# First token block by features: W_in rows and modulation columns in feature order, six GLU chunks side by side

## The chip, the cores and the metric

The kernel runs on one core of one Trainium2 chip. The metric is the device time of one execution in microseconds (us). The engines are TensorE (PE, matrix products; PEld are its weight loads), VectorE (DVE), ScalarE (ACT), GpSimd (POOL) and SyncE (SP, which issues most transfers). Each engine works through its own list of instructions in order.

## The reference

One decoder layer over 4096 tokens of 1024 features in float32 (`x` is 1 x 4096 x 1024, `c` a vector of 1024):

```python
mod = silu(c) @ w_ada + b_ada                       # 3 x 1024
shift, scale, gate = split(mod, 3)
h = layer_norm(x) * (1 + scale) + shift
u_a, z_a, glu_b, z_b = split(h @ w_in + b_in)       # 512, 512, 1024, 512 columns
pooled = causal_multiscale_pool(u_a)                # windows 2, 4, 8, 16, less the token itself
y_a = (group_linear(pooled, w_pool) + b_pool) * ls_pool * silu(z_a)
v = glu_b[..., :512] * sigmoid(glu_b[..., 512:])
v = causal_depthwise_conv31(v, w_dw) + b_dw
v = silu(layer_norm(v) * ln_conv_g + ln_conv_b)
y_b = (v @ w_pw + b_pw) * silu(z_b)
y = concat(y_a, y_b) @ w_out + b_out
out = layer_norm(alpha * x + gate * y) * ln_post_g + ln_post_b     # alpha = 2 ** 0.25
```

## The kernel before

**Tiles.** The tokens are cut into 8 blocks of 512 ("token blocks", 0 to 7; `sb` in the code). Features are cut into 8 pieces of 128 (`k`), and W_in's 2560 columns into 20 chunks of 128 (`n0`): 0 to 3 are u_a, 4 to 7 z_a, 8 to 11 and 12 to 15 the two halves of the GLU, 16 to 19 z_b. To keep float32 accuracy each operand of a product is split into a high and a low part (`split`: ACT rounds to the high part, another engine subtracts), and `mm3` makes three matmuls of 128 x 128 by 128 x 512 for each feature piece (high by high, high by low, low by high).

**Phase 1.** It loads `c`, the vectors and the columns of `w_ada`, makes shift and scale (`mod_block`: 8 `macc` instructions of DVE and a few tiny matmuls for each 256 features), turns token block 0 on PE (`make_xT`), and then makes, for each token block, four GLU pairs (chunks 8+m and 12+m, m = 0 to 3) and the chunks 16 and 17 of z_b. The weights come as column chunks (`win_chunk`: 512 KB, runs of 512 bytes); for ten of them POOL makes the low part, where the later ones have DVE do it. The modulated and split x of each block goes to DRAM (`xD`), v to `vD`. `row_stats`, `norm_T` and `mod_xT` make the x of the next token block, while PE works on the current one.

**Phase 2.** For each token block xD is loaded again (POOL's queue), and PE makes `p2z` and `p2u` for four groups and `p2b` for the chunks 18 and 19. DVE makes the pooled means (`us`, `pp`) of each group from u.

**The convolution.** It runs on DVE beside phases 1 and 2. `conv(m, s0, n, ...)` handles 128 channels of n token blocks from s0, with 31 taps folded into about 46 instructions on even and odd tokens: into `cx` (even taps) and `ca` (the result). The blocks are (0,1), (1,2), (3,2), (5,1), called block 0, 1, 3 and 5 here; token blocks 6 and 7 follow as "late units" (`la`, `lx`, `lv`) in phases 2 and 3. After the four channel groups of a block, `conv_ln` makes its LayerNorm: transposes on PE into PSUM (`cl`), statistics on ACT and DVE, a power on POOL (`ccs`), a transpose of the statistics (`ccp`), a round trip through DRAM (`cD`, read back as `cbc`), two DVE passes over `ca`, stores to `tD`. It is called after the first channel group of the next block, at high priority.

**Phase 3.** For each token block `prep` loads the normalized convolution result, applies SiLU and splits it (`vp`), and splits y_a (`ya`); `pw_stage` makes the pointwise product (`pw`) and y_b; `out_tile` makes the output product (`po`, W_out times the gate in `wor`, `wo`), the last LayerNorm and the stores.

**What sets the order.** The tiles come from pools of buffers by tag; the buffers of a tag are handed out in the order of the program text, and a tile waits until its buffer's last user is done. The tags that matter here:

- "ca", 6 buffers: `ca`, `cx`, `lx`, `vp` (and `w_ada` at the start)
- "s2b", 2 PSUM banks (`s2_bank`): `cl`, `ccp`, and in the text of before also the GLU pair m = 2 of token block 0 and `fold_u`
- "acc", 4 PSUM banks (`acc_bank`): the other products; "tpb", 2 banks: transposes and `pw`
- "wraw", 2 buffers: weights before they are split

Among the instructions whose buffers allow it, a scheduler that simulates a timeline when the program is built sets one fixed order for each engine, so work that stands late in the text (convolution, late units, phase 3) is threaded between the work of the phases.

Of the kernel before, what the change touches and what calls it, by code (L numbers as in the profile page):

```python
# [39 lines left out]
def tile_layer(ctx, tc, x, x_t, w_in_t, c, w_ada, b_ada, w_in, b_in, w_pool, b_pool, ls_pool, w_dw, b_dw,  # L40
# [75 lines left out]
    nc.vector.tensor_copy(cols, vps[:, :NV])

    wrows = s2.tile([P, P], F32, tag="cto", bufs=2, name="wrows", padded_shape=[P, T])
    nc.scalar.dma_start(wrows[: CW * MC, :], w_dw.rearrange("j o (m p) -> (j o m) p", p=P))
    wps = tp_bank("wps")  # L120
    transpose(wps[:, : CW * MC], wrows[: CW * MC, :])
# [21 lines left out]
    def wada_block(b):  # L143
        tiles = []
        for q in range(4):
            if b == 0:
                wt = wp.tile([P, 2, 2, 2 * P], F32, tag=("whi", "wlo")[q % 2], bufs=10, name=f"wa{b}_{q}")
            elif b == 1:
                wt = xp.tile([P, 2, 2, 2 * P], F32, tag="x2", bufs=12, name=f"wa{b}_{q}")
            else:  # L150
# [7 lines left out]
            tiles.append(wt)
        return tiles

    def mod_block(b, wts):
        acc = s2.tile([P, 2, 2 * P], F32, tag="bc", bufs=2, name=f"macc_{b}", padded_shape=[P, 2, DH])
        last = None
        for kt in range(KT):
            src = wts[kt // 2][:, kt % 2]
            if kt == 0:
                nc.vector.tensor_scalar(acc, src, sc[:, 0:1], None, op0=ALU.mult)
            else:
                last = nc.vector.scalar_tensor_tensor(acc, src, sc[:, kt : kt + 1], acc,
                                                      op0=ALU.mult, op1=ALU.add)  # L170
        ps = tp_bank(f"mod{b}")
        for i in range(2):
            for j in range(2):
                nc.tensor.matmul(ps[:, 2 * i + j : 2 * i + j + 1], acc[:, 1 - i, j * P : (j + 1) * P],
                                 ones[:, 0:1], start=True, stop=True)
# [4 lines left out]
        nc.vector.tensor_scalar(shn[:, k0 : k0 + 2], shc[:, k0 : k0 + 2], -1.0, None, op0=ALU.mult)  # L180
        return last

    def split(hi, lo, src, eng=nc.vector):
        nc.scalar.copy(hi, src)
        eng.tensor_tensor(lo, src, hi.bitcast(F32), op=ALU.subtract)
# [554 lines left out]
```

## Time and profile before

| | |
|---|---|
| runs | 1399.49, 1400.14, 1400.76 us; median 1400.14 |
| the profiled execution | its span is 1404.7 us, from the first to the last instruction; no other time of it is given; 4.6 us above the median |
| PE busy | 1357.8 us (97%) |
| DVE busy | 1193.9 us (85%) |
| ACT, POOL busy | 431.7 us (31%), 167.2 us (12%) |
| DMA | 243.82 MB, mean 174 GB/s |
| mean clock granted to PE | 0.991 |
| phase 1, 2, 3 on PE | first p2z at 501.26 us, first pw at 955.37 us |

Busy time is the sum of the durations of an engine's instructions; overlapping neighbours make a sum a little larger than the time they took. A row of a timeline gives the start, the duration, the engine, the line of the program, the operation, out<-in, and in brackets the idle time before it and what ended that. The lines (L333 and so on) are lines of the kernel whose profile is shown.

### The profile page before, as it was taken

The numbers are of one execution on the slowest core, as the hardware profiler recorded it, in microseconds if no ns is written. First come the engines' busy times: TensorE is split into PE (matmuls) and PEld (weight loads), VectorE is DVE, ScalarE is ACT, GpSimd is POOL, SyncE is SP. The second block draws the span as 40 slices with busy tenths as digits, with TensorE's granted clock in tenths as the row PEclk, the third lists the DMA queues.
The fourth block names the chain that finished last, engine by engine and source line by source line (L and its number), as shares of the span: only waits on it lengthen the run. The fifth ranks groups of instructions, "written<-read, shape, count | busy, mean of one in ns | idle before, by whom it ended". The sixth has DMA issues, their size and how long they took to land.

```text
span 1404.7 us, 17113 instructions
## 1 busy us (share of the span) xinstructions
PE 1357.8 (97%) x6044; PEld 1118.6 (80%) x6044; DVE 1193.9 (85%) x2318; ACT 431.7 (31%) x764; POOL 167.2 (12%) x203
## 2 busy tenths in 40 slices
PE   3989999999999999999999999989999999999997
PEld 2878888888788888888888888778888888888886
DVE  7669999983479999899898699979897899998654
ACT  3535335344531322311114111434134131322310
POOL 4310000000100011110011110410111101001111
PEclk9999999999999999999999999989999999999999
DMA  9778776567474563361440741455444443433511
GB/s 313 235 279 312 257 276 241 173 255 242 162 253 151 174 210 124 111 202 42 161 166 31 239 136 61 136 183 173 161 173 138 155 158 122 157 128 122 191 62 75
DMA packets 119496, 243.82 MB, mean 174 GB/s; under 512 B 15026, under 2 KB 52722, under 8 KB 119410
## 3 DMA queue, kind: packets, MB, share of 16 engines
q1 hardware_dynamic: 109952, 209.07, 43.4%
q0 software_dynamic: 9216, 33.56, 7.2%
q8 instruction: 47, 0.77, 0.2%
q14 instruction: 39, 0.32, 0.1%
q10 hardware_dynamic: 242, 0.10, 0.0%
HBM read 156.65 MB, written 86.04 MB: 173 GB/s over the span
## 4 chain that ended last, share of the span: by engine, by line
PE 87%; DVE 4%; DMA 4%; ACT 2%; POOL 1%; issue 1%; SPq 1%; DVEq 0%; ACTq 0%
PE po L647 25%; PE p L335 6%; PE p L334 6%; PE p L333 6%; PE p2u L333 4%; PE p2u L334 4%; PE p2u L335 4%; PE p2z L333 4%; PE p2z L335 4%; PE p2z L334 4%; PE pw L623 2%; PE pw L625 2%; PE pw L624 2%; PE p2b L333 2%; PE p2b L335 2%; PE p2b L334 2%
## 5 line engine op out<-in xcount | busy, mean ns | idle before, releaser
L510 DVE SCALAR_TENSOR_TENSOR cx<-cv,wdw,cx 128x513 f32<-128x513 f32 (+1 forms) x240 | 144.6, 611 | 0.7
L510 DVE SCALAR_TENSOR_TENSOR ca<-cx,wsum,ca 128x256 f32<-128x256 f32 (+1 forms) x240 | 143.1, 608 | 0.1
L510 DVE SCALAR_TENSOR_TENSOR ca<-cv,wdw,ca 128x256 f32<-128x256 f32 (+1 forms) x224 | 133.5, 608 | 0.0
L676 POOL TENSOR_TENSOR ors<-ove,mhalf 128x1 f32<-128x1 f32 x32 | 46.3, 1447 | 409.3 <-DVE ove L672 400.9
L326 POOL DMA_DIRECT2D x2r<-xD x64 | 34.5, 540 | 402.7 <-PE p2b L335 276.4
L670 ACT ACTIVATE ojk<-r,osm 128x1024 bf16<-128x1024 f32 x31 | 35.6, 1149 | 148.3 <-DVE osm L667 148.3
L665 DVE SCALAR_TENSOR_TENSOR r<-po,r 128x512 f32<-128x512 f32 x62 | 40.8, 685 | 23.3 <-PE po L647 23.3
L510 DVE SCALAR_TENSOR_TENSOR lx<-lv,wdw,lx 128x257 f32<-128x257 f32 x120 | 57.2, 477 | 0.0
L510 DVE SCALAR_TENSOR_TENSOR la<-lx,wsum,la 128x256 f32<-128x256 f32 x120 | 57.0, 475 | 0.0
L451 ACT ACTIVATE sz<-p2z,cols 128x512 f32<-128x512 f32 x32 | 22.0, 687 | 108.0 <-PE p2z L335 108.0
L263 POOL TENSOR_TENSOR xcs<-smx,mhalf 128x1 f32<-128x1 f32 x28 | 19.2, 688 | 290.7 <-DVE smx L262 263.9
L297 ACT ACTIVATE x<-xk,shc 128x512 fp32r<-128x512 f32 x56 | 38.5, 721 | 47.5 <-DVE xk L288 46.1
L510 DVE SCALAR_TENSOR_TENSOR la<-lv,wdw,la 128x256 f32<-128x256 f32 x112 | 52.9, 475 | 0.0
L286 DVE TENSOR_TENSOR xk<-xk,xbc 128x1024 f32<-128x1024 f32 x28 | 34.0, 1220 | 16.7 <-DMA xk<-in_x_t_dram 16.5
L263 POOL TENSOR_TENSOR ccs<-smc,mhalf 128x1 f32<-128x1 f32 x32 | 37.2, 1169 | 91.9 <-DVE smc L262 91.2
L298 DVE SCALAR_TENSOR_TENSOR x<-xk,shc,x 128x512 fp32r<-128x512 f32 x56 | 40.4, 744 | 8.1 <-ACT x L297 8.1
L458 ACT ACTIVATE u<-p2u,bu 128x512 f32<-128x512 f32 x32 | 22.0, 689 | 75.6 <-PE p2u L335 75.6
L679 DVE SCALAR_TENSOR_TENSOR r<-r,ors,b_bc 128x1024 f32<-128x1024 f32 (+1 forms) x33 | 41.0, 1246 | 3.2 <-POOL ors L676 3.1
L647 PE MATMUL po<-wo0h,ya 128*128 128x512 f32 x128 | 41.2, 392 | 0.0
L647 PE MATMUL po<-wo1h,ya 128*128 128x512 f32 x128 | 41.1, 390 | 0.0
L259 ACT ACTIVATE x<-x 128x1024 f32<-128x1024 f32 x28 | 29.6, 1059 | 35.7 <-DMA x<-in_x_dram 35.2
L639 DVE SCALAR_TENSOR_TENSOR r<-r,gbo 128x1024 f32<-128x1024 f32 x32 | 38.9, 1217 | 1.8 <-DMA r<-in_x_dram 1.8
(356 smaller groups left out, 4137.8 us busy)
## 6 DMA issues: line engine op xcount, KB each, us to landing
x2r<-xD POOLq DMA_DIRECT2D x64, 512.0 KB, 7.8
xD<-x SPq DMA_DIRECT2D x56, 512.0 KB, 6.9
x<-in_x_dram SPq DMA_DIRECT2D x32, 512.0 KB, 7.9
r<-in_x_dram SPq DMA_DIRECT2D x32, 512.0 KB, 4.4
out_dram<-r SPq DMA_DIRECT2D x31, 512.0 KB, 2.6
xk<-in_x_t_dram SPq DMA_DIRECT2D x28, 512.0 KB, 6.5
wa<-in_w_ada_dram SPq DMA_DIRECT2D x32, 256.0 KB, 4.8
wr<-in_w_in_dram SPq DMA_DIRECT2D x16, 512.0 KB, 6.5
```

Of the source, the lines that this page charges most:

```text
L263: nc.gpsimd.tensor_tensor(rstd, sm[:, 2:3], mhalf[:, 0:1], op=ALU.pow)
L297: nc.scalar.activation(h2[:, 0, :], z, AF.Identity, bias=shc[:, k : k + 1])
L298: nc.vector.scalar_tensor_tensor(h2[:, 1, :], z, shc[:, k : k + 1], h2[:, 0, :].bitcast(F32), op0=ALU.add, op1=ALU.subtract)
L333: nc.tensor.matmul(ps, wh, X[0], start=first, stop=False)
L334: nc.tensor.matmul(ps, wh, X[1], start=False, stop=False)
L335: nc.tensor.matmul(ps, wl, X[0], start=False, stop=last)
L510: nc.vector.scalar_tensor_tensor(dst, src, wt, dst, op0=ALU.mult, op1=ALU.add)
L639: xg = nc.vector.scalar_tensor_tensor(r, r, ALPHA, gbo, op0=ALU.mult, op1=ALU.add)
L647: mm = nc.tensor.matmul(po[h], lhs, Wo[k][wi][:, h * 512 : (h + 1) * 512], start=(k == 0 and wi == 0 and lhs is yh), stop=last)
L665: nc.vector.scalar_tensor_tensor(r[:, sl], po[h], 1.0, r[:, sl], op0=ALU.mult, op1=ALU.add, accum_out=sm[:, h : h + 1])
L676: nc.gpsimd.tensor_tensor(rs, ve, mhalf[:, 0:1], op=ALU.pow)
L679: nc.vector.scalar_tensor_tensor(r[:, sl], r[:, sl], rs, b_bc[:, sl], op0=ALU.mult, op1=ALU.add)
```

## The change

1. At first only `b_ada` and `b_in` are loaded (2 transfers on ACT's queue). The other vectors, `w_dw` and the correction constants come after token block 0's products (`late_vectors`, on SP's queue).
2. The shift and scale columns of `w_ada` come in five blocks of 1, 1, 2, 2 and 2 feature pieces in place of four blocks of 2, into other buffers.
3. The GLU weights come as 8 rows of 128 features by 1024 columns (`load_row`, runs of 4 KB) in place of 8 column chunks, and are split row by row, in two pieces of 768 and 256 columns. The chunks of z_b that phase 1 needs come as two tiles (`Wz`).
4. All these low parts are made on DVE.
5. Token block 0: for each feature piece, six GLU chunks (8, 12, 9, 13, 10, 14) take their three products one after the other, in four banks of "acc" and two of "s2b". The pair m = 3 and z_b follow.
6. Token block 7, the last of phase 1: z_b first, then the pair m = 0, then the pairs 1, 2 and 3 side by side, the pair m = 2 in the two banks of "s2b".
7. The buffers of the gate and of `gbo` hold W_in rows first.

```diff
-    for nm, src, n in (("b_ada", b_ada, 24), ("b_in", b_in, 20), ("b_pool", b_pool, 4),
-                       ...
-        nc.scalar.dma_start(vrows[r0 : r0 + n, :], view)
+    load_cols((("b_ada", b_ada, 24), ("b_in", b_in, 20)), nc.scalar.dma_start, "a")
...
-    def split(hi, lo, src, eng=nc.vector):
+    def split(hi, lo, src):
         nc.scalar.copy(hi, src)
-        eng.tensor_tensor(lo, src, hi.bitcast(F32), op=ALU.subtract)
+        nc.vector.tensor_tensor(lo, src, hi.bitcast(F32), op=ALU.subtract)
...
-    def load_pair(m):
-        W[8 + m] = win_chunk(8 + m, nc.gpsimd)
-        W[12 + m] = win_chunk(12 + m, nc.gpsimd)
-
-    wad = [wada_block(0)]
-    load_pair(0)
+    def load_row(k):
+        home = k % 4
+        rows[k] = (wraw(f"wr{k}") if home < 2 else
+                   cst.tile([P, D], F32, tag=("gate", "gbo")[home - 2], name=f"wr{k}"))
+        nc.sync.dma_start(rows[k], w_in[k * P : (k + 1) * P, 8 * P : 16 * P])
+
+    mods = ((0, 1), (1, 1), (2, 2), (4, 2), (6, 2))
+    wad = []
+    for b, (k0, nk) in enumerate(mods):
+        wad.append(wada_tiles(b, k0, nk))
+        for k in range(k0, k0 + nk):
+            load_row(k)
...
     xT = []
-    for b in range(4):
-        if b < 3:
-            wad.append(wada_block(b + 1))
-            load_pair(1 + b)
-        last = mod_block(b, wad[b])
-        xT += make_xT(0, xt_next, range(2 * b, 2 * b + 2))
+    first = (8, 12, 9, 13, 10, 14)
+    pss0 = [acc_bank(f"p1_0_{n0}") for n0 in first[:4]] + [s2_bank(f"p1_0_{n0}") for n0 in first[4:]]
+    starts = {k0: b for b, (k0, nk) in enumerate(mods)}
+    mod_block(0, *mods[0], wad[0])
+    pb = turn_x(xt_next, 0)
+    for k in range(KT):
+        xT.append(mod_turned(pb, k))
+        split_cols(k, 0, 3)
+        split_cols(k, 3, 4)
+        if k + 1 < KT:
+            if k + 1 in starts:
+                b = starts[k + 1]
+                last = mod_block(b, *mods[b], wad[b])
+            pb = turn_x(xt_next, k + 1)
+        for n0, ps in zip(first, pss0):
+            mm3(ps, W[n0][k], xT[k], k == 0, k == KT - 1)
+    late_vectors()
...
     for sb in range(NSB):
...
-        for m in range(MC):
-            pa, pg = inproj(xT, (W[8 + m], W[12 + m]), f"p1_{sb}_{m}",
-                            s2_bank if sb == 0 and m == 2 else acc_bank)
...
+        if sb + 1 == NSB:
+            z_half(sb, xT)
+            glus(sb, (0,), xT, (acc_bank,) * 2)
+            glus(sb, (1, 2, 3), xT, (acc_bank,) * 2 + (s2_bank,) * 2 + (acc_bank,) * 2)
+            break
+        if sb == 0:
+            for m in range(3):
+                glu(0, m, pss0[2 * m], pss0[2 * m + 1])
+        for m in range(3 if sb == 0 else 0, MC):
+            glus(sb, (m,), xT, (acc_bank,) * 2)
```

The change also moves instructions that no line of the diff names. The rows below are the fixed order of one engine: line, operation, out<-in, size. A number behind a name's parts is a buffer number (`cl0_2_6720` is the transpose tile 2 of convolution block 0's LayerNorm; `p1_5_3_1` is token block 5, m = 3, second of the pair; `p1_7_15` in the changed kernel is token block 7, chunk 15; `ca5_3` is block 5, channel group 3; `us7_3_0` is token block 7, group 3).

PE, LayerNorm of convolution block 0. Before, rows 1452 to 1458 of PE, in token block 5's GLU of phase 1 (its first transposes are rows 479 and 480):

```order
L334 MATMUL p1_5_3_1_2831<-x2_5_6_2607,w15h_553 128x512
L77 MATMUL cl0_2_6720<-ident_75,ca0_0_6412 128x128
L77 MATMUL cl0_2_6720<-ident_75,ca0_1_6469 128x128
L77 MATMUL cl0_2_6720<-ident_75,ca0_2_6526 128x128
L77 MATMUL cl0_2_6720<-ident_75,ca0_3_6583 128x128
L77 MATMUL cl0_3_6731<-ident_75,ca0_0_6412 128x128
L77 MATMUL cl0_3_6731<-ident_75,ca0_1_6469 128x128
```

After, rows 1982 to 1984, the end of phase 1 and the start of phase 2, followed shortly by the transposes (rows 1998 to 2003):

```order
L337 MATMUL p2z_0_0_3743<-x2r_0_5_3737,w4h_3669 128x512
L338 MATMUL p2z_0_0_3743<-x2r_0_5_3737,w4h_3669 128x512
L73 MATMUL cl0_0_6731<-ident_75,ca0_0_6445 128x128
L73 MATMUL cl0_0_6731<-ident_75,ca0_1_6502 128x128
L73 MATMUL cl0_0_6731<-ident_75,ca0_2_6559 128x128
L73 MATMUL cl0_0_6731<-ident_75,ca0_3_6616 128x128
```

The last GLU product of phase 1 (`p1_7_15`) is row 1982 and the first `p2z` row 1983, so the transposes of block 0 moved from phase 1 into phase 2.

DVE, the convolution in phase 1. After, rows 507 to 513: the last tap of `cx1_1` is row 509, and the next instruction of a convolution is row 627, behind block 0's LayerNorm (rows 616 to 625):

```order
L576 SCALAR_TENSOR_TENSOR cx1_1_6798<-cv1_1_6796,wdw_99,cx1_1_6798 128x513
L268 TENSOR_SCALAR smx23_2307<-smx23_2307 128x1
L576 SCALAR_TENSOR_TENSOR cx1_1_6798<-cv1_1_6796,wdw_99,cx1_1_6798 128x513 x9
L445 SCALAR_TENSOR_TENSOR v4_1_2437<-p1_4_9_2385,cols_92,sg4_1_2435 128x512
L292 TENSOR_TENSOR xk5_0_2320<-xk5_0_2320,xbc5_2318 128x1024
L294 SCALAR_TENSOR_TENSOR xk5_0_2320<-xk5_0_2320,s1_281,xbc5_2318 128x512 x2
L292 TENSOR_TENSOR xk5_2_2325<-xk5_2_2325,xbc5_2318 128x1024
```

So 89 rows without a tap of the convolution stand there now (510 to 598), up to the end of phase 1.

DVE, the end of convolution block 5. Before, rows 1370 to 1379, with a late unit and the pooled mixer of token block 6 beside it:

```order
L519 TENSOR_TENSOR ca5_3_7569<-ca5_3_7569 128x256
L510 SCALAR_TENSOR_TENSOR la6_0_7691<-lx6_0_7693,wsum_138,la6_0_7691 128x256
L510 SCALAR_TENSOR_TENSOR lx6_0_7693<-lv6_0_7692,wdw_136,lx6_0_7693 128x257
L510 SCALAR_TENSOR_TENSOR la6_0_7691<-lv6_0_7692,wdw_136,la6_0_7691 128x256
L510 SCALAR_TENSOR_TENSOR la6_0_7691<-lv6_1_7748,wdw_136,la6_0_7691 128x256
L470 TENSOR_TENSOR us6_3_0_6009<-u6_3_6004 128x263
L471 TENSOR_TENSOR us6_3_0_6009<-u6_3_6004 128x263
L482 SCALAR_TENSOR_TENSOR pp6_2_5948<-pp6_2_5948,bpl_326,sz6_2_5909 128x512
L520 SCALAR_TENSOR_TENSOR ca5_3_7569<-cx5_3_7570,cols_130,ca5_3_7569 128x256
L510 SCALAR_TENSOR_TENSOR la6_0_7691<-lx6_0_7693,wsum_138,la6_0_7691 128x256
```

Rows 1503 and 1504 of before hold token block 7's last pooled group:

```order
L687 TENSOR_TENSOR wor5_7894<-wor5_7894,gate_bc_324 128x1024
L480 SCALAR_TENSOR_TENSOR pp7_2_6282<-us7_2_2_6280,u7_2_6272 128x512
L470 TENSOR_TENSOR us7_3_0_6341<-u7_3_6338 128x263
L471 TENSOR_TENSOR us7_3_0_6341<-u7_3_6338 128x263
L185 TENSOR_TENSOR wo4l_7891<-wor4_7887,wo4h_7890 128x1024
```

After, that group (rows 1307 and 1308) stands ahead of the end of block 5 (row 1452):

```order
L546 SCALAR_TENSOR_TENSOR pp7_2_6315<-us7_2_2_6313,u7_2_6305 128x512
L536 TENSOR_TENSOR us7_3_0_6374<-u7_3_6371 128x263
L537 TENSOR_TENSOR us7_3_0_6374<-u7_3_6371 128x263
L576 SCALAR_TENSOR_TENSOR cx5_2_7546<-cv5_2_7544,wdw_99,cx5_2_7546 128x257
L576 SCALAR_TENSOR_TENSOR ca5_2_7545<-cv5_2_7544,wdw_99,ca5_2_7545 128x256
L576 SCALAR_TENSOR_TENSOR ca5_2_7545<-cx5_2_7546,wsum_100,ca5_2_7545 128x256
```

and block 5's end, rows 1448 to 1453:

```order
L585 TENSOR_TENSOR ca5_3_7602<-ca5_3_7602 128x256
L576 SCALAR_TENSOR_TENSOR la6_0_7724<-lv6_1_7781,wdw_99,la6_0_7724 128x256
L576 SCALAR_TENSOR_TENSOR la6_0_7724<-lx6_0_7726,wsum_100,la6_0_7724 128x256
L576 SCALAR_TENSOR_TENSOR lx6_0_7726<-lv6_0_7725,wdw_99,lx6_0_7726 128x257
L586 SCALAR_TENSOR_TENSOR ca5_3_7602<-cx5_3_7603,cols_92,ca5_3_7602 128x256
L576 SCALAR_TENSOR_TENSOR la6_0_7724<-lv6_1_7781,wdw_99,la6_0_7724 128x256
```

The two have changed places: `us7_3_0` came 125 rows behind the last instruction of `ca5_3` and comes 145 rows ahead of it now.

PE, the boundary of phases 2 and 3. Before, rows 3742 and 3743 transpose `ca5_3` (in `p2b` of token block 6, with 259 rows up to the first `pw`), and the boundary itself, rows 3998 to 4003, is:

```order
L333 MATMUL p2b_7_3_0_6382<-x2r_7_7_6092,w19h_3690 128x512
L334 MATMUL p2b_7_3_0_6382<-x2r_7_7_6092,w19h_3690 128x512
L335 MATMUL p2b_7_3_0_6382<-x2r_7_7_6092,w19l_3691 128x512
L623 MATMUL pw0_0_7919<-vp0_0_7822,wpw0h_7809 128x512
L624 MATMUL pw0_0_7919<-vp0_0_7822,wpw0h_7809 128x512
L625 MATMUL pw0_0_7919<-vp0_0_7822,wpw0l_7810 128x512
```

After, rows 3985 to 3995 (the last row of `p2u_7_3` is 3939, and rows 3940 to 3987 are `p2b`):

```order
L337 MATMUL p2b_7_3_6415<-x2r_7_7_6125,w19h_3723 128x512
L338 MATMUL p2b_7_3_6415<-x2r_7_7_6125,w19h_3723 128x512
L339 MATMUL p2b_7_3_6415<-x2r_7_7_6125,w19l_3724 128x512
L73 MATMUL cl5_0_7659<-ident_75,ca5_1_7488 128x128
L73 MATMUL cl5_1_7670<-ident_75,ca5_1_7488 128x128
L73 MATMUL cl5_0_7659<-ident_75,ca5_2_7545 128x128
L73 MATMUL cl5_1_7670<-ident_75,ca5_2_7545 128x128
L73 MATMUL cl5_0_7659<-ident_75,ca5_3_7602 128x128
L73 MATMUL cl5_1_7670<-ident_75,ca5_3_7602 128x128
L73 MATMUL cl5_2_7681<-ident_75,ca5_0_7317 128x128
L73 MATMUL cl5_2_7681<-ident_75,ca5_1_7488 128x128
```

The transposes of block 5 now stand between `p2b` and `pw`, and PE can't pass them before `ca5_3` is done.

More of the change, by code (lines that the diff above doesn't have):

```diff
@@ L112, in tile_layer @@
-    NV = r0
-    vps = tp_bank("vps")
-    transpose(vps[:, :NV], vrows[:NV, :])
-    cols = cst.tile([P, NV], F32, name="cols")
[L116 to L121, printed above, removed]
+    col, NV = {}, 0
+    for nm, n in (("b_ada", 24), ("b_in", 20), ("b_pool", 4), ("ls", 4), ("b_dw", 4), ("lncg", 4),
+                  ("lncb", 4), ("b_pw", 4)):
+        col[nm] = NV
+        NV += n
@@ new lines, in tile_layer, with load_cols @@
+    cols = cst.tile([P, NV], F32, name="cols")
+    def load_cols(srcs, dma, name):
+        rows = s2.tile([P, P], F32, tag="cto", bufs=2, name=f"vrows{name}", padded_shape=[P, T])
+        r0 = 0
+        for nm, src, n in srcs:
+            dma(rows[r0 : r0 + n, :], src if nm == "b_pool" else src.rearrange("(r p) -> r p", p=P))
+            r0 += n
+        vps = tp_bank(f"vps{name}")
+        transpose(vps[:, :r0], rows[:r0, :])
+        c0 = col[srcs[0][0]]
+        nc.vector.tensor_copy(cols[:, c0 : c0 + r0], vps[:, :r0])
@@ new lines, in tile_layer @@
+    late_vectors()
+    Wz = []
+    for q in range(2):
+        raw = wraw(f"wzr{q}")
+        nc.sync.dma_start(raw.rearrange("p (k n) -> p k n", k=4),
+                          w_in[q * 512 : (q + 1) * 512, 16 * P : 18 * P].rearrange("(k p) n -> p k n", p=P))
+        Wz.append(wslot(f"wz{q}"))
+        split(*Wz[q], raw)
+    for m in range(2):
+        W[16 + m] = []
+        for k in range(KT):
+            a = (k % 4) * 2 * P + m * P
+            W[16 + m].append((Wz[k // 4][0][:, a : a + P], Wz[k // 4][1][:, a : a + P]))
@@ L387, in tile_layer @@
+    gate_bc = cst.tile([P, D], F32, tag="gate", name="gate_bc")
+    gbo = cst.tile([P, D], F32, tag="gbo", name="gbo")
     for k in range(KT):
@@ L389, in tile_layer, with glu, glus, z_half @@
             after(nc.sync.dma_start(xD[k][0][:, i, :], xT[k][i].bitcast(F32)), last, True)
+    def glu(sb, m, pa, pg):
+        sg = ph.tile([P, T], F32, tag="sg", bufs=2, name=f"sg{sb}_{m}")
+        nc.scalar.activation(sg, pg, AF.Sigmoid, bias=vec("b_in", 12 + m))
+        v = ph.tile([P, T], F32, tag="v", bufs=2, name=f"v{sb}_{m}")
+        nc.vector.scalar_tensor_tensor(v, pa, vec("b_in", 8 + m), sg, op0=ALU.add, op1=ALU.mult)
+        nc.sync.dma_start(vD[m][sb].rearrange("p two i -> p (two i)"), v)
+    def glus(sb, ms, xT, banks):
+        ns = [n0 for m in ms for n0 in (8 + m, 12 + m)]
+        pss = inproj(xT, ns, [f(f"p1_{sb}_{n0}") for f, n0 in zip(banks, ns)])
+        for i, m in enumerate(ms):
+            glu(sb, m, pss[2 * i], pss[2 * i + 1])
+    def z_half(sb, xT):
+        for m in range(2):
+            (pz,) = inproj(xT, (16 + m,), [acc_bank(f"p1z_{sb}_{m}")])
+            sg = ph.tile([P, T], F32, tag="sg", bufs=2, name=f"sgz{sb}_{m}")
+            nc.scalar.activation(sg, pz, AF.Silu, bias=vec("b_in", 16 + m))
+            nc.sync.dma_start(zD[0][sb][:, m, :], sg)
     for sb in range(NSB):
```

179 lines of the change are left out of this document (87 added, 92 removed).

## The prediction

> **What bounds the kernel now.** I read the page first, then the list of what TensorE (PE) waited for, then windows along the span, then the timelines of the places where PE stood still. The page:
>
> ```profile
> span 1404.7 us, 17113 instructions
> PE 1357.8 (97%) x6044; PEld 1118.6 (80%) x6044; DVE 1193.9 (85%) x2318; ACT 431.7 (31%) x764; POOL 167.2 (12%) x203
> PE   3989999999999999999999999989999999999997
> DVE  7669999983479999899898699979897899998654
> PE 87%; DVE 4%; DMA 4%; ACT 2%; POOL 1%; issue 1%; SPq 1%; DVEq 0%; ACTq 0%
> ```
>
> PE is busy 97% of the span and is 87% of the chain that ended last; its row of slices falls below 9 at the start and at one place in the second half. VectorE (DVE) has 85%, with a hole in slices 9 and 10. So two things can move the time: what PE loses at its few stops, and anything that makes PE wait for DVE, which has little to spare. The stops, as a list of what PE waited for (us in total, times, longest):
>
> ```profile
> PE vps L77 <- DMA vrows<-in_b_pw_dram: 8.8, 1, 8.8
> PE mod L174 <- DVE macc L169: 8.7, 3, 5.1
> PE ccp L77 <- POOL ccs L263: 7.3, 1, 7.3
> PE p L334 <- DVE x L317: 3.0, 1, 3.0
> PE fv L352 <- DMA wT<-in_w_in_t_dram: 2.3, 2, 1.5
> ```
>
> All but ccp lie in the first 104 us. Windows (us, then busy time of PE, weight loads, DVE, ACT, POOL, each with its count, clock, DMA share, GB/s):
>
> ```profile
> 300.00:400.00 100.00, 97.82 (x436) 79.99 (x435) 43.18 (x78) 45.90 (x81) 6.57 (x12) 1.00 0.62 215
> 400.00:500.00 100.00, 100.00 (x444) 82.75 (x443) 98.11 (x145) 30.61 (x36) 4.92 (x9) 1.00 0.56 187
> 500.00:900.00 400.00, 400.00 (x1804) 331.19 (x1803) 370.38 (x747) 86.60 (x207) 47.58 (x74) 1.00 0.40 135
> 900.00:960.00 60.00, 52.75 (x223) 43.00 (x222) 51.53 (x94) 22.55 (x37) 12.66 (x3) 0.91 0.52 166
> ```
>
> From 300 to 400 DVE is idle for 56.8 us, since the convolution's tiles are held until the LayerNorm (LN) of block 0 has run; from 400 to 900 PE has no gap, while DVE works 468.5 of 500 us. What DVE doesn't do before 500 it can hardly do before 955, where phase 3 begins.
>
> **The start.** Rows of before's timeline (start, duration, [idle before <- releaser]):
>
> ```profile
> 22.22 0.79 PE L333 MATMUL p<-x,w8h 128*128 128x512 f32 x1
> 26.49 0.79 PE L334 MATMUL p<-x,w8h 128*128 128x512 f32 x1 [3.05 <-DVE x L317]
> 34.96 1.73 PE L174 MATMUL mod<-ones,macc 128*128 128x1 f32 x8 [3.06 <-DVE macc L169]
> 97.21 1.95 PE L352 MATMUL fv<-wpl,wT 128*128 128x128 f32 x16
> 101.15 0.50 PE L333 MATMUL p<-x,w8h 128*128 128x512 f32 x1 [1.79 <-ACT x L297]
> 17.73 0.75 DVE L169 SCALAR_TENSOR_TENSOR macc<-wa,sc,macc 128x512 f32<-128x512 f32 x1
> 27.67 4.33 DVE L169 SCALAR_TENSOR_TENSOR macc<-wa,sc,macc 128x512 f32<-128x512 f32 x3
> 28.64 2.81 POOL L185 TENSOR_TENSOR w9l<-wr,w9h 128x1024 fp32r<-128x1024 f32 x1 [4.72 <-ACT w9h L184]
> 901.35 1.20 DVE L185 TENSOR_TENSOR wpw0l<-pwr,wpw0h 128x1024 fp32r<-128x1024 f32 x1
> ```
>
> The new start wants one feature of modulation and one W_in row before the first product, and does six chunks with each feature. It removes two stops of 3.05 and 3.06 us; the vector load carries two DMAs in place of nine, so vps can only come sooner. From the loads' order I put PE's first product near 19.5 and the first of token block 1 near 93 against 101.15: **-8 us**. This is an estimate; the ends are -16 (all 17 us of waits between 2 and 35 us gone except the first loads' landing) and +2 (each stop comes back at a feature whose weight row is late). The ten splits taken from GpSimd (POOL, 2.81 us each) cost DVE 10 x 1.13 = 11.3 us (1.20 less the 0.07 by which neighbours overlap). The macc instructions that run beside a POOL split are slow: three took 4.33 us where one takes 0.75, so 2.1 too much; over seven such places up to 14 us comes back. I book 0 for DVE, with -3 to +11. The late vectors and the correction constants are wanted only by the convolution and phase 2, past 100 us: nothing. Later allocation of the gate and of gbo: nothing, since the same loads are only issued later and phase 3 alone needs them.
>
> In the Trainium skill, "SBUF — State Buffer", section "SBUF: two separate sides", says that DVE and GpSimd share a port pair as an exclusive lock, held for a whole instruction by whoever starts first. The 4.33 us row beside the 2.81 us split agrees.
>
> **The last token block of phase 1.** Here the diff looks harmless: z first, then GLU 0, then GLU 1 to 3 side by side, two of the six in the banks of the tag s2b. There are only two of these, taken in turn in program order, and the LN of the convolution uses them too. So the LN of block 0 (cl, then ccp) now stands behind token block 7's GLU. The order shows it: its transposes, rows 479 to 1460 of PE before (done at 386.42 of the timeline below), are now rows 2000 to 2007, after phase 2 has begun. PE loses nothing there by itself. DVE does: four of the six "ca" slots hold block 0's results until that LN, conv (1,1) stops at its first part, and rows 511 to 598 of DVE hold no convolution at all, only 66.6 us of other work (counted by form, with durations as below) for the time from token block 4's second GLU to the end of phase 1, 175 us at least (three blocks of the 57 us that a block takes between 101 and 501). Before, the hole was 56.8 us; now it is about 105, so about 50 us of convolution, and its LN's chain, move into phase 2. Phase 2 has (500 to 955) some 36 us of DVE idle time. That does not fit.
>
> **The boundary of phases 2 and 3.** Before:
>
> ```profile
> 884.51 0.47 DVE L520 SCALAR_TENSOR_TENSOR ca<-cx,cols,ca 128x256 f32<-128x256 f32 x1
> 904.88 12.54 POOL L263 TENSOR_TENSOR ccs<-smc,mhalf 128x1 f32<-128x1 f32 x2 [4.76 <-DVE smc L262]
> 378.02 1.22 POOL L263 TENSOR_TENSOR ccs<-smc,mhalf 128x1 f32<-128x1 f32 x2
> 386.42 0.27 PE L77 MATMUL ccp<-ident,ccs 128*8 128x128 f32 x1
> 399.24 2.50 DVE L540 TENSOR_TENSOR ca<-ca,cbc 128x512 f32<-128x512 f32 x4 [8.59 <-DMA cbc<-cD]
> 501.26 0.40 PE L333 MATMUL p2z<-x2r,w4h 128*128 128x512 f32 x1
> 917.47 0.38 PE L77 MATMUL ccp<-ident,ccs 128*8 128x128 f32 x1 [7.25 <-POOL ccs L263]
> 918.07 0.63 PE L334 MATMUL p2u<-x2r,wu1h 128*128 128x512 f32 x1
> 922.68 0.40 PE L333 MATMUL p2z<-x2r,w6h 128*128 128x512 f32 x1
> 924.68 2.49 DVE L540 TENSOR_TENSOR ca<-ca,cbc 128x512 f32<-128x512 f32 x4
> 955.14 0.39 PE L335 MATMUL p2b<-x2r,w19l 128*128 128x512 f32 x1
> 955.37 0.39 PE L623 MATMUL pw<-vp,wpw0h 128*128 128x512 f32 x1
> ```
>
> Block 5's last convolution ended at 885, 70 us before phase 3, and pw followed p2b without a wait. The one loss is 7.25 us for ccp and then half speed (pitch 0.43 instead of 0.227) until 922.68, 2.4 us: together 9.7.
>
> After, PE's row 3992 transposes ca5_3, and 3939 is the last row of p2u_7_3. Between them PE has 48 matmuls of 0.227, 10.9 us. On DVE, row 1307 (us7_3_0) needs u7_3, so p2u_7_3; ca5_3's last instruction is row 1452. DVE runs in order, so all 146 rows of 1307 to 1452 lie between, whatever came before. Their forms (count | busy, mean ns):
>
> ```profile
> L510 DVE SCALAR_TENSOR_TENSOR ca<-cv,wdw,ca 128x256 f32<-128x256 f32 x112 | 52.3, 474 | 0.0
> L540 DVE TENSOR_TENSOR ca<-ca,cbc 128x512 f32<-128x512 f32 x8 | 5.0, 684 | 8.6 <-DMA cbc<-cD 8.6
> L541 DVE SCALAR_TENSOR_TENSOR ca<-ca,cols,cbc 128x512 f32<-128x512 f32 x8 | 5.5, 748 | 0.0
> L687 DVE TENSOR_TENSOR wor<-wor,gate_bc 128x1024 f32<-128x1024 f32 x8 | 9.7, 1217 | 0.0
> ```
>
> 110 taps of 256 elements x 0.397 (0.474 less an overlap of 0.077) = 43.7; seven of 1024 elements x 1.13 = 7.9; the 29 others, by size, 10.7: together 62.3. With 0.9 from the end of p2u_7_3 to row 1307 (ACT's u) DVE finishes at 63.2 at the earliest, PE arrives at 10.9, so PE waits **+52 us** (63.2 - 10.9). It is more if DVE comes late to 1307. By PE's own path phase 2 begins at 493 (501.26 less 8) and takes 955.14 - 501.26 - 9.7 = 444 us, so PE stands at ca5_3 from 937 and ca5_3 ends at 990. By DVE's path it ends at 885 + 50 of moved convolution + about 50 for what stands ahead of row 1452 now and stood behind row 1378 before (parts of two late units, products of W_out with the gate, the pooled mixer of block 7): 985, an estimate. The two bounds meet, and I add nothing.
>
> What is late next: call X the end of ca5_3. vp0_0's split, row 1489, is 11.4 us of DVE work after X; before it PE can't start pw. ccp stands behind the first two pw rows; from ccp to the LN's first instruction the trace has 7.2 us (917.47 to 924.68) and 12.8 (386.42 to 399.24), so that comes at X + 20 or later. Rows 1501 to 1533, 18.1 us with four instructions of 0.684 and four of 0.748, hold the rest of the LN, ya0_0, without which no po starts (at about X + 29), and the last vp0 at X + 38. In these 38 us PE can do 57 matmuls, 13 us. Loss 25, +2 for a cold restart (2.4 above), +2 for POOL: **+29 us**. Ends: 22 (some of rows 1518 to 1533 don't hold PE) and 45 (the two pow take 12.54 us in place of 1.22, and ccp to LN 12.8 in place of 7.2).
>
> By the same rule of the Trainium skill a pow loses the port for one DVE instruction, at most 1.3 us here, and this term would be 27. The trace has 12.54 us for two pow beside an unbroken run of DVE, so the rule gives only the low side. In "TensorE: Matmul & The Clock Gate", Part 1, the skill has half clock for about 3.4 us after an idle window; by that a restart costs 1.7, the trace's 5.2 us of half speed 2.4.
>
> **Sum.** Start -8; old ccp stop gone, since another order stands there, -9.7; boundary wait +52; after X +29; other stops in phase 2 (LN of blocks 0, 1 and 3, each again at one ccp, of which one in three cost 9.7 before) +3: +66.3. The profiled execution gives 1404.7 + 66.3 = 1471.0; it was 4.6 above the median of the runs (1400.14), so **1466 us**.
>
> **The rivals.**
> - *More.* DVE arrives late at row 1307, because the convolution that moved costs it more than the 36 us free there, or POOL is starved as at 904.88. For: the DVE row of phase 2; against: the two bounds meet. The worse ends (+16) give 1482, another 15 us of late DVE 1497. Chance 0.12.
> - *Less.* PE waits at row 3988, but after X the tail is hidden, and the start gives its best: +52 + 22 - 16 - 9.7 = +48.3, 1448. For: PE has po and pw mixed there. Chance 0.13.
> - *The other side: faster.* If ca5_3 ends before p2b_7_3, there is no wait, and only -8 and -9.7 remain: 1382. It decides at 52 us: DVE would have to do rows 1307 to 1452 in under 11 us, or the order on the chip would not be the built one. Against: rows in order and 110 taps at 0.397. Chance 0.04.
> - *The start doesn't do what it says*, because six chunks by feature want 0.5 MB of weights for each: +8 on the forecast, 1474, inside the main case.
>
> **How the numbers follow.** Main case 0.70 with 1455 to 1482 (the ends of the start and of the POOL term), more 0.12, less 0.13, faster 0.04, within 0.2% (2.8 us, about what a measurement of this kernel can tell) 0.01. The range leaves out the last two and about half of each end: 1440 to 1495. Slower 0.95, same 0.01, faster 0.04.
>
> **What the profile after would show.** PE gapless to about the 26th slice, then one wait of about 50 us at cl <- DVE ca (L586), and waits for vp, ya and cbc in the 30 us behind it; DVE with a hole of about 105 us before the end of phase 1 and none in phase 2; the first product at about 19.5 us and token block 1 from about 93; no macc slower than 0.8 us. Wrong it is if PE goes from p2b to cl without a wait, or if DVE's row us7_3 comes after the end of ca5_3.

## The result, and the profile after

The changed kernel takes 1476.68 us (median of 4 runs, 1474.07 to 1476.93) against 1400.45 us in the same comparison: a ratio of 1.0518, 95% interval 1.0479 to 1.0557. The prediction was 1466 us in 1440 to 1495. The profiled execution's span is 1474.3 us, 69.6 more than before's. One execution of the version below called "Less convolution at the boundary" took 1980.64 us at a granted clock of 0.677, where its other three had 0.964 to 0.966, so its time is given from those three.

The page of the changed kernel: span, busy times, and the slices of PE, DVE and of the clock granted to PE:

```profile
span 1474.3 us, 17147 instructions
PE 1360.5 (92%) x6045; PEld 1119.7 (76%) x6045; DVE 1196.1 (81%) x2348; ACT 430.6 (29%) x770; POOL 130.6 (9%) x193
PE   4979999999999999999999999503999999999997
DVE  8598989864331389999999989999999799998654
PEclk9989999999999999999999999855999999999999
```

PE has the same work (1360.5 against 1357.8 us) and a single new gap, in slices 25 to 27 (counted from 0). DVE has its hole in slices 9 to 13 instead of 9 and 10. The list of what PE waited for:

```profile
PE cl L73 <- DVE ca L586: 56.5, 3, 32.0
PE mod L186 <- DVE macc L181: 11.9, 2, 10.0
PE po L713 <- ACT ya L195: 9.2, 1, 9.2
PE fv L358 <- DMA wT<-in_w_in_t_dram: 5.7, 2, 4.5
PE pw L689 <- ACT vp L195: 3.7, 1, 3.7
```

The first line is new and is most of the loss; `po` and `pw` are what came late behind it. Windows of the changed kernel (columns as in the prediction):

```profile
300.00:400.00 100.00, 100.00 (x443) 82.58 (x442) 40.53 (x67) 40.79 (x65) 4.38 (x8) 1.00 0.65 228
400.00:500.00 100.00, 100.00 (x442) 82.79 (x442) 32.00 (x37) 27.22 (x33) 6.63 (x12) 1.00 0.54 182
500.00:955.00 455.00, 442.41 (x1993) 365.99 (x1991) 416.08 (x756) 103.51 (x232) 43.86 (x72) 0.99 0.38 127
955.00:1010.00 55.00, 4.65 (x16) 2.94 (x16) 54.76 (x148) 6.40 (x18) 1.66 (x3) 0.50 0.21 68
```

From 400 to 500 DVE worked 98.11 us before and works 32.00 now. From 300 to 500 together it does 68.8 us less than before and stands idle for 127.5 us. That is the convolution which did not run, and at 955 it is still owed: for 55 us DVE works with hardly a gap (54.76) and PE does 4.65 us. DVE did not lack time in between: from 500 to 955 it stood idle for 38.9 us, about as long as before (36.7), since its next row in order was waiting for something else (for ScalarE's pass over `cl` 10.3 us, for `u` 9.1, for `cbc` 8.0). From 897.3 us on it has no such wait. The timelines of PE and DVE:

```profile
97.12 1.23 PE L337 MATMUL p<-x,wg0h 128*128 128x512 f32 x4 [2.10 <-ACT x L303]
497.07 0.39 PE L337 MATMUL p2z<-x2r,w4h 128*128 128x512 f32 x1
942.02 0.39 PE L339 MATMUL p2b<-x2r,w19l 128*128 128x512 f32 x1
962.04 0.69 PE L73 MATMUL cl<-ident,ca 128*128 128x128 f32 x2 [19.63 <-DVE ca L586]
967.53 0.69 PE L73 MATMUL cl<-ident,ca 128*128 128x128 f32 x2 [4.80 <-DVE ca L586]
1000.25 0.69 PE L73 MATMUL cl<-ident,ca 128*128 128x128 f32 x2 [32.03 <-DVE ca L586]
1009.38 1.22 PE L689 MATMUL pw<-vp,wpw0h 128*128 128x512 f32 x2 [3.70 <-ACT vp L195]
1024.03 1.22 PE L713 MATMUL po<-wo0h,ya 128*128 128x512 f32 x2 [9.17 <-ACT ya L195]
```

```profile
300.84 0.75 DVE L576 SCALAR_TENSOR_TENSOR cx<-cv,wdw,cx 128x513 f32<-128x513 f32 x1
527.47 0.48 DVE L574 TENSOR_SCALAR ca<-cv,wdw 128x512 f32<-128x512 f32 x1
937.83 0.44 DVE L536 TENSOR_TENSOR us<-u 128x263 f32<-128x263 f32 x1
999.71 0.48 DVE L586 SCALAR_TENSOR_TENSOR ca<-cx,cols,ca 128x256 f32<-128x256 f32 x1
```

No tap of the convolution runs between 301.6 and 527.5 us; before, the same hole ended at 412.5. PE ends `p2b` at 942.25 (the start of its last matmul and one pitch of 0.227) and stands, with two short turns, until `ca5_3` is done at 1000.2; full work begins with `po` at 1024 to 1028.

### The profile page after: what moved, and what is told of

Its sections match the earlier page's. It is cut to its first block, busy times and chain, and to the rows that moved or that the text cites. A ratio compares the mean times of both kernels' runs of the same rounds, so it can differ in the third digit from the quotient of the medians.

```text
span 1474.3 us, 17147 instructions
## 1 busy us (share of the span) xinstructions
PE 1360.5 (92%) x6045; PEld 1119.7 (76%) x6045; DVE 1196.1 (81%) x2348; ACT 430.6 (29%) x770; POOL 130.6 (9%) x193
## 4 chain that ended last, share of the span: by engine, by line
PE 88%; DVE 6%; DMA 4%; SPq 1%; issue 1%; ACT 0%; POOL 0%; DVEq 0%; ACTq 0%
PE po L713 24%; PE p L338 8%; PE p L339 8%; PE p L337 7%; PE p2z L337 4%; PE p2z L338 4%; PE p2z L339 4%; PE p2u L337 4%; PE p2u L338 4%; PE p2u L339 4%; PE pw L689 2%; PE pw L691 2%; PE p1z L339 2%; PE p1z L338 2%; PE p1z L337 2%; PE pw L690 2%
## 5 line engine op out<-in xcount | busy, mean ns | idle before, releaser
L576 DVE SCALAR_TENSOR_TENSOR cx<-cv,wdw,cx 128x257 f32<-128x257 f32 (+1 forms) x240 | 146.0, 614 | 0.9
L73 PE MATMUL cl<-ident,ca 128*128 128x128 f32 x96 | 16.2, 296 | 59.2 <-DVE ca L586 56.5
L73 PEld LDWEIGHTS cl<-ident,ca 128*128 128x128 f32 x96 | 12.4, 151 | 63.2 <-DVE ca L586 57.7
L445 DVE SCALAR_TENSOR_TENSOR v<-p,cols,sg 128x512 f32<-128x512 f32 x32 | 23.8, 748 | 41.1 <-ACT sg L443 39.5
L304 DVE SCALAR_TENSOR_TENSOR x<-xk,shc,x 128x512 fp32r<-128x512 f32 x56 | 39.8, 745 | 13.3 <-ACT x L303 13.2
L269 POOL TENSOR_TENSOR ccs<-smc,mhalf 128x1 f32<-128x1 f32 x32 | 25.2, 795 | 210.6 <-DVE smc L268 204.4
```

The costliest lines, as they stand in the source:

```text
L269: nc.gpsimd.tensor_tensor(rstd, sm[:, 2:3], mhalf[:, 0:1], op=ALU.pow)
L304: nc.vector.scalar_tensor_tensor(h2[:, 1, :], z, shc[:, k : k + 1], h2[:, 0, :].bitcast(F32), op0=ALU.add, op1=ALU.subtract)
L576: nc.vector.scalar_tensor_tensor(dst, src, wt, dst, op0=ALU.mult, op1=ALU.add)
```

## The experiments

**One word: other banks in token block 7.**

```diff
-            glus(sb, (1, 2, 3), xT, (acc_bank,) * 2 + (s2_bank,) * 2 + (acc_bank,) * 2)
+            glus(sb, (1, 2, 3), xT, (acc_bank,) * 2 + (tp_bank,) * 2 + (acc_bank,) * 2)
```

> The changed kernel with one word changed: in token block 7 the GLU pair m = 2 takes the two banks of the tag tpb in place of s2b; all else of the change stays. Theory 'held bank' (the LayerNorm of convolution block 0 stands behind token block 7 because of the two s2b banks): the LayerNorm is back in phase 1, no PE wait for ca at the boundary, the hole of DVE ends near 400 us again, and only the 4.2 us of the start remain: 1396 us (1390 to 1400). Rival 'fuller DVE' (the ten splits taken from GpSimd and the new start make DVE late at the boundary): still over 1460. Rival 'side by side' (z first and three pairs side by side in token block 7 set the late order, whatever the bank): still over 1460.

Measured: 1403.35 us, ratio 0.9974 (0.9942 to 1.0006). The loss, 73 us, is gone and the wait for `ca` with it. Its windows and its longest waits:

```profile
300.00:400.00 100.00, 99.39 (x444) 81.58 (x444) 43.52 (x78) 45.48 (x81) 6.58 (x12) 1.00 0.62 216
```

```profile
PE mod L186 <- DVE macc L181: 11.2, 2, 9.6
PE ccp L73 <- POOL ccs L269: 6.9, 1, 6.9
PE fv L358 <- DMA wT<-in_w_in_t_dram: 4.5, 1, 4.5
```

"Fuller DVE" and "side by side" fall: splits, new start, z first and three pairs side by side are all still there. The median is 3 above the upper end given, because the runs fall in two groups, 1394.2 to 1397.6 (5) and 1402.8 to 1408.3 (7); more on that below. The kernel before has two groups in this comparison, too: 13 runs from 1397.9 to 1402.8 and 10 from 1408.8 to 1416.5. Lower group against lower group, this version is 4 us faster (medians 1395.5 and 1399.4).

**The converse: only the bank, in the kernel before.**

```diff
-                            s2_bank if sb == 0 and m == 2 else acc_bank)
+                            s2_bank if sb in (0, NSB - 1) and m == 2 else acc_bank)
```

> The kernel before with one edit: in token block 7, too, the pair m = 2 of the GLU takes the banks s2b; no new start, no new splits, the pairs one after the other and z last as before. 'Held bank': the whole loss appears without the rest of the change: on DVE 57 us of work from the last pooled group to the end of ca5_3, less 10.9 of PE's own work, plus some 6 that DVE comes late, plus 25 behind it, less 9 for the old stop at ccp: +69, 1469 us (1455 to 1485). 'Fuller DVE' and 'side by side': 1400, no change.

Measured: 1474.32 us, ratio 1.0482 (1.044 to 1.0523). One condition on one line of the kernel before makes the whole loss; 1469 was expected. Its wait:

```profile
PE cl L77 <- DVE ca L520: 54.1, 3, 29.6
```

**The new start alone, token block 7 as the others.** The special case of the last block is taken out; pairs one after the other, then z.

> The changed kernel with token block 7 done like the others (pairs one after the other in acc, then z): the new start alone. 'Held bank': as with the banks tpb, 1396 us (1390 to 1400), and within 3 us of it, since the order of token block 7 costs nothing by itself. 'Side by side': 1396 here too, but then the version with banks tpb is slow. 'Fuller DVE': over 1460.

Measured: 1397.6 us, ratio 0.9957 (0.992 to 0.9995), again in two groups (1393.2 to 1398.1, 6 runs; 1404.5 to 1409.1, 4 runs). The lower groups of this version and of the one with banks tpb lie about 1 us or less apart at both ends, so the order of token block 7 costs nothing by itself, as expected.

**The LayerNorm moved, the bank of token block 7 kept.** If the loss came from using s2b in token block 7, this would not help; if it came from block 0's LayerNorm standing behind it, it would.

```diff
-            pb = s2_bank(f"cl{s0}_{q}")
+            pb = (tp_bank if s0 == 0 else s2_bank)(f"cl{s0}_{q}")
...
-        to_rows(s2_bank(f"ccp{s0}"), cs, ...
+        to_rows((tp_bank if s0 == 0 else s2_bank)(f"ccp{s0}"), cs, ...
```

> The changed kernel as it is, with pair m = 2 of token block 7 in s2b, but the LayerNorm of convolution block 0 alone (cl and ccp) takes the banks tpb. 'Held bank': what counts is that block 0's LayerNorm no longer stands behind token block 7; in the order it is back in phase 1 (PE rows 1503 to 1564), and the end of ca5_3 comes ahead of the last pooled group again: 1400 us (1392 to 1415), PE waits at the boundary under 15 us. 'Side by side' or any cost of s2b in token block 7 itself: still over 1460.

Measured: 1403.27 us, ratio 1.0015 (0.9995 to 1.0036). Behind 500 us two short waits are left, the first at the boundary (950 us), the second at 695 us:

```profile
PE po L713 <- ACT ya L195: 4.6, 1, 4.6
PE cl L73 <- DVE ca L586: 0.7, 1, 0.7
```

So it is the place of the LayerNorm in the rotation of the two banks, shown from three sides.

**Less convolution at the boundary.** `EARLY = 0` and `PERSB = (2, 2, 1, 1, 1, 1, 0, 0)` in the changed kernel.

> The changed kernel with the convolution of token block 6 (two late units) written after the start of phase 3 in place of before it (EARLY = 0, and two units in each of the first two blocks of phase 3). In the built order DVE then has 50.5 us of work from the last pooled group to the end of ca5_3 in place of 62.3, and 17 us from there to the last vp in place of 33.8. 'Held bank', with the wait made of the DVE rows in between: the PE wait at the boundary is about 12 us shorter and the part behind it 10 to 17 shorter: 1450 us (1442 to 1460). If the wait were set by DVE's sum of work and not by the rows in between, the time stays within 5 us of 1476.

Measured: 1481.96 us (median of 1481.86, 1481.96 and 1486.01), ratio 1.0544 (1.0494 to 1.0594): a miss of 32 us, and the wrong way. The wait at the boundary shrank as expected, the part behind it hardly, and the end took back more than both:

```profile
987.05 0.69 PE L73 MATMUL cl<-ident,ca 128*128 128x128 f32 x2 [17.76 <-DVE ca L586]
1008.11 1.22 PE L713 MATMUL po<-wo0h,ya 128*128 128x512 f32 x2 [11.89 <-ACT ya L195]
1424.90 1.22 PE L689 MATMUL pw<-vp,wpw0h 128*128 128x512 f32 x2 [14.27 <-ACT vp L195]
```

`ca5_3` is done 13.2 us earlier (987.05 against 1000.25); `po` starts 15.9 earlier (1008.11 against 1024.03), so the part behind gave 2.7 up to there, where 10 to 17 were expected. And the late units now end at 1401, token block 7's LayerNorm runs behind them, and PE, with nothing else left, waits 14.3 us for `vp` (and 3.0 for its `ccp`) near the end. The expectation had counted what left the boundary, and not who waited for the units that moved. For the wait itself the run speaks for the rows in between, whose work was cut by 11.8 us in the order, and not for DVE's sum of work.

**Small tiles parted.** What held block 0's LayerNorm until some 378 us before (its first powers on GpSimd start at 378.02) were two kinds of small tiles which both LayerNorms take in turn. They were given to each apart, in the version with banks tpb and in the kernel before:

```diff
-        sm = st.tile([P, 3], F32, tag="sm", bufs=4, ...
+        sm = st.tile([P, 3], F32, tag="sm" + name[0], bufs=4 if name[0] == "c" else 3, ...
-        rows = st.tile([n, P], F32, tag="rows8", bufs=2, ...
+        rows = st.tile([n, P], F32, tag="rows" + name[0], bufs=1, ...
```

> The version with banks tpb in token block 7, and in it the small tiles of the LayerNorms parted: sm (4 for the convolution, 3 for x) and rows8 (one each) in place of shared ones. In the order, block 0's LayerNorm now stands in token block 3 of phase 1 (DVE row 481 in place of 573), and block 5's last PE transposes 370 PE rows earlier. 'Held bank' in general form (what holds the ca buffers decides when the convolution can run): DVE's hole from 300 to 400 is filled, the convolution ends some 40 to 50 us earlier, and since PE bounds the time only the stop at ccp can go: 1387 us (1380 to 1398). Rival: DVE's place in phases 1 and 2 doesn't matter as long as PE doesn't wait for it, and the stop at ccp comes back at another place: within 3 us of the version with banks tpb.

> The kernel before, with the same two kinds of small tiles parted (sm, rows8) and nothing else. First theory: -9.7 from the stop at ccp: 1391 us (1384 to 1401). Rival: no change, 1400.

Measured: 1397.85 us, ratio 0.997 (0.9952 to 0.9988), and 1401.49 us, ratio 1.0005 (0.9994 to 1.0017). The windows of the second one:

```profile
300.00:400.00 100.00, 97.97 (x426) 79.74 (x425) 99.97 (x160) 36.80 (x57) 5.43 (x6) 0.98 0.49 171
500.00:955.00 455.00, 455.00 (x2032) 376.31 (x2031) 384.55 (x765) 106.90 (x223) 42.62 (x74) 1.00 0.43 145
```

DVE's hole is filled (99.97 us of 100 in place of 43.18), the stop at `ccp` is gone (455.00 of 455 in place of 447.75), block 0's first powers come at 250.18, and the median hasn't moved. The gain of 9.7 us that the first theory saw in the stop did not come: of the two expectations for the kernel before, 'no change' held. What did come is that the runs of both versions keep together: all 12 within 4.1 and within 3.6 us.

**The low parts of the W_in rows on GpSimd again**, in the version with banks tpb: for all eight rows, and for rows 2 to 7 alone (`eng=nc.gpsimd if k > 1 else nc.vector` in `split_cols`).

> The version with banks tpb in token block 7, and in it the low parts of the eight W_in rows made by GpSimd again, as the kernel before made them. The prediction booked 0 for moving these splits (-3 to +11): within 4 us of the version with banks tpb. If the splits on DVE were dear, 5 to 10 us faster; if GpSimd slows the macc beside it, as in the kernel before, the first product stays near 21 us and later features come late: 3 to 8 us slower.

> The version with banks tpb, with GpSimd making the low parts of rows 2 to 7 and DVE those of rows 0 and 1, which stand right before the first products. If GpSimd's split slows the macc of the third modulation block (seven took 9.08 us beside it, and PE waited 4.8 us for them), 2 to 4 us faster than with all rows on GpSimd: 1390 us (1387 to 1395). If DVE's 11 us of splits are what costs, nothing gained: 1393 to 1396.

Measured: 1393.49 us, ratio 0.9953 (0.9935 to 0.9971; 11 runs from 1389.67 to 1394.70 and one of 1404.93), and 1390.88 us, ratio 0.993 (0.9908 to 0.9953; 6 runs, 1389.64 to 1393.46). The second is the fastest version found, faster than both kernels. The first was expected within 4 us of the version with banks tpb: its median lies 9.9 below, its lower group 2. With all rows on GpSimd the macc beside its splits are slow, and PE waits for them:

```profile
23.29 9.08 DVE L181 SCALAR_TENSOR_TENSOR macc<-wa,sc,macc 128x512 f32<-128x512 f32 x7
```

```profile
PE mod L186 <- DVE macc L181: 9.5, 1, 9.5
PE mod L186 <- DVE shc L190: 4.8, 1, 4.8
```

Seven took 9.08 us, 1.3 each where they start some 0.67 apart when DVE is left alone. With rows 0 and 1 on DVE that second wait is gone, and the wait for `fv` is 0.5 us, against 1.7 with all rows on GpSimd and 4.5 with all on DVE.

What the new start is worth shows where token block 2 begins. The rows are PE's first product of token block 2 in the kernel before, in the changed kernel, and in the version with rows 2 to 7 on GpSimd; the last is the wait of the changed kernel in token block 1:

```profile
167.19 0.39 PE L333 MATMUL p<-x,w8h 128*128 128x512 f32 x1
168.13 0.62 PE L337 MATMUL p<-x,wg0h 128*128 128x512 f32 x2
161.77 0.62 PE L337 MATMUL p<-x,wg0h 128*128 128x512 f32 x2
107.72 3.75 PE L358 MATMUL fv<-wpl,wT 128*128 128x128 f32 x16 [4.50 <-DMA wT<-in_w_in_t_dram]
```

In the six traces that have the new start and all splits on DVE, token block 2 begins at 166.1 to 169.0 us; in the four with the start of the kernel before (two profiles of it and two versions of it) at 166.2 to 170.4; in the four with the rows on GpSimd, all or six of them (two come next), at 160.9 to 162.9. So up to there the new start gains nothing in these traces as long as DVE makes the low parts, and some 6 us when GpSimd does.

**Parted tiles on top of these two.**

> The version with banks tpb and the W_in rows' low parts on GpSimd (1393.5 us), with the small tiles of the two LayerNorms parted too. Theory 'the stop at ccp comes only in some executions, and where the runs of a kernel fall in two groups some 10 us apart, it is that stop': parting removes the upper group and hardly moves the lower one: all runs within 5 us, median 1393 (1390 to 1396). Rival 'the stop is in every execution': 5 to 10 us faster, 1384 to 1388.

> Both: banks tpb, rows 2 to 7 on GpSimd, small tiles parted. The sum of the two: 1390 us (1386 to 1395), all runs within 5 us, and the fastest of the versions if the start and the stop at ccp are independent.

Measured: 1397.56 us, ratio 0.9981 (0.9967 to 0.9995), and 1396.01 us, ratio 0.9967 (0.9954 to 0.9981): all 12 runs within 3.1 and 4.1 us, and 4 to 5 us slower than without parting. That the runs keep together was expected; both expectations of a median near 1390 to 1393 missed. The traces of both show one new wait of about that size, at 334 us: with DVE busy for 192 and 194 of the 200 us from 300 to 500, the x of the next token block comes late (3.6 us in the first, 3.8 in the second). Whether it is the whole difference isn't shown.

```profile
PE p L338 <- DVE x L304: 4.4, 2, 3.6
```

By that reading the kernel's hole on DVE was no pure loss: it kept DVE free for the work that PE waits for next.

**The kernel before, profiled a second time.**

> The kernel before, unchanged, profiled a second time. If the stop at ccp (7.25 us idle, 2.4 us of half speed in the first profile) is there only in some executions, this profile either has it, at a span near 1404.7, or lacks it, at a span of 1395 to 1399, which is then what the median of 1400 belongs to. If it is in every execution, it is here again and the span is within 2 us of 1404.7.

Measured: one run of 1407.92 us, span 1406.2 us, with the stop, of the same length:

```profile
896.23 5.21 POOL L263 TENSOR_TENSOR ccs<-smc,mhalf 128x1 f32<-128x1 f32 x2 [6.85 <-DVE smc L262]
906.21 12.52 POOL L263 TENSOR_TENSOR ccs<-smc,mhalf 128x1 f32<-128x1 f32 x2 [4.77 <-DVE smc L262]
```

Both outcomes were open with the stop there, so this run alone does not decide. But it took 1407.92 us, and it is the run that was profiled: the stop goes with a long run. In all listed runs of the kernel before, the time is 1.7 to 1.9 us longer than the span, so the first profile, with its span of 1404.7, belongs to a run of about 1406.5 us (an estimate) and not to one like the three listed ahead of the prediction. In the comparisons with many runs of the kernel before, 13, 30 and 22 of them lie from 1396.7 to 1403.6, and 10, 5 and 1 from 1407.2 to 1416.5. So the reading is that the stop comes only in some executions, and that the median of 1400 belongs to those without it.

Two kept traces speak for it more than the parted versions do (all 12 runs of each of these in one group, where the kernel before itself has only 5 of 35 and 1 of 23 in the upper one). The last powers of block 5 with banks tpb, with all rows on GpSimd, and with rows 2 to 7 on GpSimd, none of them parted:

```profile
906.40 12.53 POOL L269 TENSOR_TENSOR ccs<-smc,mhalf 128x1 f32<-128x1 f32 x2 [8.14 <-DVE smc L268]
902.72 2.31 POOL L269 TENSOR_TENSOR ccs<-smc,mhalf 128x1 f32<-128x1 f32 x2 [8.15 <-DVE smc L268]
899.31 2.31 POOL L269 TENSOR_TENSOR ccs<-smc,mhalf 128x1 f32<-128x1 f32 x2 [8.14 <-DVE smc L268]
```

The profiled runs took 1407.51, 1394.70 and 1390.38 us: the first lies in the upper group of its version and has the stop, the second lies in the lower group of its version, the third belongs to a version whose six runs all lie below 1393.5, and PE does not wait for `ccp` in either. The trace of the new start alone (1404.49 us, upper group) has the stop again: 12.93 us for two powers, 7.9 us of waiting. DVE's rows beside the powers stand in a slightly different order with the rows on GpSimd, and no profile of the kernel before without the stop was caught, so for that kernel the reading stays argued and not shown.

## Why the prediction was right, point by point

- **The boundary wait, +52.** It was 58.0 (942.25 to 1000.25). The term's core was right to a tenth: from DVE's `us7_3_0` to the end of `ca5_3` 62.3 us were summed from the forms, and 62.4 passed (937.83 to 1000.19). What was 6 too small is the arrival: DVE reached `us7_3_0` 6.5 us after the end of `p2u_7_3` (931.37), not 0.9; it had had no gap since 897.3. The two bounds that "meet", 990 and 985, both lay ahead of the measured 1000.2, and the one by DVE's path rested on sizes that were off: the hole was 127.5 us of idle DVE and not 105, the work that it moved 68.8 us and not 50. Nor was the wait decided by how much free time DVE had in phase 2: it left 38.9 us unused. The order of the rows decided.
- **Behind X, +29.** It was 24.7: from the end of `p2b` to the end of the program 532.05 us against 449.33 before is 82.7, less 58.0. GpSimd's powers were not starved there (2.18 us for two, not 12.54), and the path from `ccp` to the LayerNorm took 5.7 us (1011.96 to 1017.65), not 7.2 or 12.8. By the lock rule of the Trainium skill ("SBUF — State Buffer", "SBUF: two separate sides") the low side, an estimate of 27, was the nearer one here; the 12.5 us of the kernel before, seen in both its profiles, remain beyond what one lost turn explains.
- **The old stop at ccp, -9.7, and +3 for other stops.** In the profile phase 2 took 445.2 us in place of 454.1: -8.9, against -6.7 summed. PE had no gap in it, so the +3 did not come.
- **The start, -8.** This is the term that was mis-sized most. Token block 1 began 4.0 us earlier (97.12 against 101.15), and in it the gain was lost: PE waited 5.7 us for `fv`, where it was 2.3 before, and token block 2 began 0.9 us later than before. The step that failed is the booking of 0 for the splits moved to DVE: with rows 2 to 7 on GpSimd, and nothing else changed in the version with banks tpb, the wait for `fv` is 0.5, token block 2 begins at 161.77 in place of 169.01, and the time falls by some 4.5 us (1390.88 against the lower group's 1394.2 to 1397.6 with banks tpb). The end of -16 rested on 17 us of waits between 2 and 35 us; the five of them sum to 21.3.
- **The rest of phase 1, put at nothing.** Phase 2 began 4.2 us earlier all the same (497.07 against 501.26). From token block 2 on, phase 1 took 5.1 us less, 4.0 of it in token block 5 (54.55 in place of 58.53 us), where block 0's LayerNorm had stood. It left phase 1 for the bank's sake, and not because of the start.
- **Against the span, and against the median.** The sum was +66.3, the spans differ by 69.6, and the medians by 76.2. That the sum came within 3.3 us of the spans is in part luck: the misses of +6.0 (boundary), -4.3 (behind X), +8.9 (start), -5.1 (rest of phase 1) and -2.2 (phase 2) nearly cancel. The other 6.6 us come from laying a difference from the profiled execution on the median: that execution was some 6 us longer than the median run (about 1406.5, by the estimate above, against 1400.14), and the changed kernel's was not (1476.43 against 1476.68). If the stop is in the profiled execution and not in the median run, as argued above, the -9.7 was no gain for the median, and without it the sum gives 1400 + 66.3 + 9.7 = 1476. With the terms as measured the same reckoning gives 1400 + 69.6 + 9.7 = 1479, so it holds to some 3 us.
- **The rivals.** No other case came: PE waited, and the order on the chip was the built one. Of the forecast's last list the wait at `cl`, the waits behind it and the macc held; the first product came at 20.85 instead of 19.5 and token block 1 at 97.1 instead of 93, the hole was 127.5 us and not 105, and phase 2 had idle time on DVE where none was expected.

## What to carry to other kernels

Two PSUM banks handed out in program order tie together whatever takes them: before a tile goes into a spare bank, list who else takes that tag later in the text, and what that one holds in turn (here: banks, then a LayerNorm, then four of six buffers, then some 69 us of DVE's work). Where engines run a fixed order, as here, a wait of 50 us can be read from the order and the durations alone: find the last row that needs the waiting engine, the first row that it will wait for, and sum the rows in between (62.3 summed, 62.4 measured). Look at where a gain is lost again, not only where it is made: here a lead of 4 us at token block 1 was gone at token block 2. And look at the spread of the runs before taking a stop in one profiled execution for a stop in the median.

## What the runs showed of the hardware

- Two powers of 128x1 on GpSimd take 1.22 us at 378 us of the kernel before. Beside a run of two-input DVE instructions without a gap they took 12.5 to 12.9 us in four traces (the kernel before twice, banks tpb, the new start alone), but 2.31 us in two others (rows on GpSimd), and 2.18 in another place of the changed kernel with as busy a DVE. What decides between these isn't shown.
- A DVE macc of 512 elements takes 0.75 us, 1.3 on average beside GpSimd's splits. Making the low parts of six of eight rows on GpSimd in place of DVE was worth some 4.5 us here; whether the two rows whose neighbours PE waits for are better on DVE (1390.88 against 1393.49) is not clear of noise: the intervals of the two ratios overlap.
